# A two-layer encoder trunk: output blocks evicted later, gate rows activated together, a tenth Strassen pair, products on a constant

## The chip, the cores and the metric

One core of a Trainium2 chip runs the whole program. The metric is device time in microseconds (us); the kernel before takes 2105.63 us as the median of three runs (2105.11 to 2105.88).

## The reference

Two batches, 256 and 512 positions, go through one even and one odd layer with the same weights; together they are T = 768 rows of D = 2048. What matters here is the even layer:

```python
def _even_layer(x, g, w_in, w_out, q_gain, k_gain, sink, w_f, b_f, rel_bias):
    z = _rmsnorm(x, g) @ w_in
    q, k, v, f, ga, gf = _split(z, EVEN_SPLITS)          # 1536, 512, 512, 512, 1536, 512
    q = _rmsnorm(q.reshape(B, S, N_HEADS, HEAD_DIM), q_gain)
    k = _rmsnorm(k.reshape(B, S, N_KV_HEADS, HEAD_DIM), k_gain)
    ...
    a = _window_attention(q, k, v, rel_bias, sink) * jax.nn.silu(ga)
    fo = _fourier(f...).reshape(B, S, FOURIER_WIDTH) * jax.nn.silu(gf)
    return x + jnp.concatenate([a, fo], axis=-1) @ w_out
```

The attention looks 128 positions to either side, with 12 heads in 4 groups of 3, a bias and a sink logit. The odd layer has one input projection, a gated convolution, a spatial gate and `x + concat @ w_out` again. All is fp32.

## The kernel before

**Products.** Every fp32 operand is kept as a high and a low part: `split` (L133) casts the high part on ScalarE and subtracts it on VectorE for the low part. A product is three matmuls (`three`, L123): high by high, high by low, low by high. Operands lie with features on partitions, a row block is 128 x 768 in two halves of H = 384 columns; most matmuls are 128x128 by 128x384.

**Weights.** `Weights` holds a ring of four split weight tiles (`wh`, `wl`, 128x512), which `weights.ahead` fills a few tiles ahead, in one list `order` of all tiles of the program. For a Strassen pair `source` (L196) makes the sums of weight quarters on VectorE, in place (L204 to L210).

**Strassen pairs.** `strassen` (L486) multiplies two blocks of 128 output features by all 2048 inputs with seven products of 24 matmuls, 168 in place of 192. The first product is copied out of its bank (`r1`, L508); the others are combined by VectorE, and each of the four results goes to a *sink*: `Normed` (queries and keys), `Gates` (two blocks of the FNet gate, SiLU on ScalarE, then to memory) or `Out`.

**Order in time.** TensorE's order is the order of the Python code, with a planner on top: `Pipe` keeps a clock that each matmul moves on by its columns, generators are spawned with a delay, and `pipe.tick()` runs those that are due; `pipe.flush()` runs all that are left. The other engines get their instructions in the order in which the code issues them, moved by a framework's scheduler.

**Stages (us).** 0 to 75: the FNet projection `f`, with the rows of x loaded, split (`split_gain`, L277) and squared, the squares added on GpSimd (L559). To 165: a double block of FNet gates and the values. To 460: nine pairs `pairs_in`, eight of them queries and keys and the ninth two FNet gates. To 537: FNet, with three attention gate blocks between its products. 537 to 755: attention. To 850: four plain output blocks as two double blocks (`Out.run`, L434), then output pairs. Then the odd layer, with the same `Out.run` at 1850 to 2102.

**Attention gates.** `ga_block` (L700) multiplies one block of 128 gate features (96 matmuls), applies SiLU on ScalarE straight from the two banks (L704) and writes the row to memory. Three run in the FNet stage, nine as filler between the attention's units. The attention has 24 units (4 groups by 6 blocks of 128 queries), each a generator `attend` (L875), spawned every `UNITS_AT` = 8.0 of the planner's clock: load and split of the query (`qh`), scores with scaling (L896) and maximum, exponentials (L908, L910), division, transposes with casts (`pth`, L923), the product with the values and the copy into `at` (L933). After a group's last unit `gates` (L867) loads the three gate rows and multiplies them into `at` (`gate`).

**Output.** `Out.run` spawns `build_sums`, which makes the Strassen sums of the left operand on VectorE while the two double blocks run; after each double block it evicts its four halves at once: residual load, addition from the bank (L458), result (`keep_sum`, L952, with a square on ScalarE L958 and an addition on GpSimd L959). Then `pipe.flush()` runs what is left of the sums, and the pairs begin.

Of the kernel before, what the change touches and what calls it, by code (L numbers as in the profile page):

```python
# [17 lines left out]
P = 128  # L18
# [7 lines left out]
H = T // 2  # L26
# [16 lines left out]
FIRST_UNIT, UNITS_AT = 13.0, 8.0  # L43
PT_AT, PV_AT = 9.0, 14.2
PE = mybir.EngineType.PE
# [50 lines left out]
def trunk(ctx, tc, x_t, w_in_e, w_fn, w_vn, w_out_e, w_in_o, w_sv, w_out_o, w_f, w_st, b_s, sink, rel_bias,  # L96
# [58 lines left out]
    rr = const.tile([P, T], F32, name="rr")  # L155
    rt = const.tile([P, NT], F32, name="rt")
# [70 lines left out]
    pairs_in = [tuple(norms[i:i + 2]) for i in range(0, len(norms), 2)] + [(GF0 + 2, GF0 + 3)]  # L227
# [11 lines left out]
    order += [(w_in_e, 0, GA0 + j, q) for j in range(NQ) for q in (QLATE if j == 0 else range(4))]  # L239
# [184 lines left out]
    class Out:  # L424
# [7 lines left out]
        def run(self):  # L432
            st = Stream(self.n)

            def load(k, h, t):
                nc.sync.dma_start(out=t, in_=cat[k][:, SL[h]])

            ready = set()

            def refill(j):  # L440
                if j in ready:
                    fill(j, 1, s4d[j])
                ready.add(j)

            def done(k, s):
                if s == 1 and k < KH:
                    refill(k)

            pipe.spawn(build_sums(load, sums, BUILD, BUILD_AT, done=refill), BUILD_FROM)
            for i, tags in zip(range(0, len(PLAIN), 2), self.tags):  # L450
                duo = PLAIN[i:i + 2]
                last = i + 2 == len(PLAIN)
                st.duo(duo, tags, done if last else None, range(4) if i else self.qs)
                for b in duo:
                    for h, z in enumerate(st.take(b)):
                        res = ev()
                        nc.sync.dma_start(out=res, in_=self.res[b][:, SL[h]])
                        nc.vector.tensor_add(out=res, in0=z, in1=res)  # L458
                        self.result(b, h, res)
            pipe.flush()  # L460
            for b in self.pairs:
                self.r = [big(i)[:, :T] for i in range(2)]
                for r, c in zip(self.r, b):
                    nc.sync.dma_start(out=r, in_=self.res[c])
                lent[0] = b != self.pairs[-1]
                strassen(self.n, b, sums, ev, self, self.tags[-1])
            lent[0] = False

# [132 lines left out]
    with tc.tile_pool(name="early", bufs=1, reuse_waits="tile") as pool:  # L601
# [62 lines left out]
        class Gates:  # L664


            def keep(self, b, h, t, src=None):
                nc.scalar.activation(out=t, in_=t if src is None else src, func=AF.Silu)
                nc.sync.dma_start(out=gs_d[b - GF0][:, SL[h]], in_=t)
# [14 lines left out]
        for b in pairs_in:  # L684
            strassen(0, b, sums, ev, Gates() if b[0] >= GF0 else Normed(), (6, 2, 7, 3))
# [13 lines left out]

    def ga_block(j, tile):  # L700
        z = st.block(GA0 + j, QLATE if j == 0 else range(4))
        g = tile()
        for s in range(2):
            nc.scalar.activation(out=g[:, SL[s]], in_=z[s], func=AF.Silu)  # L704
        nc.sync.dma_start(out=ga_d[j], in_=g)

    with tc.tile_pool(name="fnet", bufs=1, reuse_waits="tile") as pool:
# [115 lines left out]
        for j in range(3):  # L823
            ga_block(j, lambda: pool.tile([P, T], F32, name="gated"))
# [3 lines left out]
    with tc.tile_pool(name="attn", bufs=1, reuse_waits="tile") as pool:  # L828
        rows.append(pool)

        class Group:


            def __init__(self, g):
                self.g = g

# [30 lines left out]
            def gates(self):  # L867
                g = self.g
                rs = []
                for j in range(3):  # L870
                    rs.append(row_tile())
                    nc.sync.dma_start(out=rs[j], in_=ga_d[3 * g + j])
                    gate(rs[j], 3 * g + j, self.at[:, j, :], g == NKV - 1)

        def attend(gr, s, qb):  # L875
# [58 lines left out]
            if (s, qb) == (1, SEQS[1][1] - 1) and g < NKV - 1:  # L934
                yield 1.0
                gr.gates()
# [8 lines left out]
        for j in range(3, NQ):  # L945
            ga_block(j, row_tile)
        pipe.flush()
        gr.gates()
# [255 lines left out]
```

## Time and profile before

| | us |
|---|---|
| median of three runs | 2105.63 |
| profiled execution | 2104.2 |
| its span | 2102.4 |
| TensorE busy | 2078.6 (99%) |
| VectorE busy | 1469.0 (70%) |
| ScalarE busy | 1000.9 (48%) |
| GpSimd busy | 75.5 (4%) |
| mean granted TensorE clock | 0.998 |

The profile is of one execution. Busy time is the union of an engine's instructions; the rest of the span the engine was idle. A row of the waits view names the engine, its line, what released it, the total, how often and the longest. In a timeline row the bracket at the end is the idle time before the instruction and what ended it; x2 joins like instructions in a row.

### The profile page before, as it was taken

The numbers are of one execution on the slowest core, as the hardware profiler recorded it, in microseconds if no ns is written. First come the engines' busy times: TensorE is split into PE (matmuls) and PEld (weight loads), VectorE is DVE, ScalarE is ACT, GpSimd is POOL, SyncE is SP. The second block draws the span as 40 slices with busy tenths as digits, with TensorE's granted clock in tenths as the row PEclk, the third lists the DMA queues.
The fourth block names the chain that finished last, engine by engine and source line by source line (L and its number), as shares of the span: only waits on it lengthen the run. The fifth ranks groups of instructions, "written<-read, shape, count | busy, mean of one in ns | idle before, by whom it ended". The sixth has DMA issues, their size and how long they took to land.

```text
span 2102.4 us, 32021 instructions
## 1 busy us (share of the span) xinstructions
PE 2078.6 (99%) x11712; PEld 2019.0 (96%) x11712; DVE 1469.0 (70%) x2605; ACT 1000.9 (48%) x1979; POOL 75.5 (4%) x75
## 2 busy tenths in 40 slices
PE   8999999999999998999999999999999999999999
PEld 6989999999999998999888999999999999999999
DVE  8686677764566787667975666666667777796665
ACT  6345545553788864335444333333334555643332
POOL 5000000000000001211000000000000000000000
PEclk9999999999999999999999999999999999999999
DMA  6895323354444385446854222222222233494342
GB/s 225 244 301 180 101 89 91 110 173 148 133 149 149 118 282 195 145 128 196 292 206 149 85 81 88 70 74 81 88 88 82 93 108 106 145 304 157 119 129 76
DMA packets 158342, 303.55 MB, mean 144 GB/s; under 512 B 16316, under 2 KB 107624, under 8 KB 158184
## 3 DMA queue, kind: packets, MB, share of 16 engines
q1 hardware_dynamic: 158184, 301.51, 44.8%
q8 instruction: 92, 1.51, 0.3%
q14 instruction: 66, 0.54, 0.1%
HBM read 240.08 MB, written 64.51 MB: 145 GB/s over the span
## 4 chain that ended last, share of the span: by engine, by line
PE 82%; DMA 6%; DVE 5%; ACT 4%; issue 2%; SPq 1%; POOL 0%; DVEq 0%; ACTq 0%; POOLq 0%
PE bank L120 82%; DMA slot<-cat 1%; DVE slot L135 1%; DVE slot L280 1%; DVE wl L135 1%; DMA wr<-in_w_out_o_dram 1%; ACT slot L134 1%; DMA xr<-in_x_t_dram 1%; PE bank L130 1%; ACT wh L134 1%; DMA s<-slot 0%; ACT slot L279 0%; ACT L704 0%; ACT sc L908 0%; DMA row<-f_d 0%
## 5 line engine op out<-in xcount | busy, mean ns | idle before, releaser
L120 PE MATMUL bank<-slot,wh 128*128 128x384 f32 x6448 | 1647.1, 336 | 5.8 <-ACT wh L134 3.6
L120 PEld LDWEIGHTS bank<-slot,wh 128*128 128x128 f32 x6448 | 1164.5, 188 | 9.6 <-ACT wh L134 3.9
L120 PE MATMUL bank<-slot,wl 128*128 128x384 f32 x3224 | 1083.9, 336 | 1.4 <-DVE wl L135 1.3
L134 ACT CAST wh<-wr 128x512 fp32r<-128x512 f32 x782 | 480.9, 621 | 722.9 <-PE bank L120 543.8
L135 DVE TENSOR_TENSOR wl<-wr,wh 128x512 fp32r<-128x512 f32 x782 | 541.3, 697 | 305.7 <-ACT wh L134 297.3
L120 PEld LDWEIGHTS bank<-slot,wl 128*128 128x128 f32 x3224 | 606.2, 188 | 2.6 <-DVE wl L135 2.6
L120 PE MATMUL bank<-wh,slot 128*128 128x512 f32 x768 | 242.2, 395 | 5.7 <-ACT slot L279 5.5
L134 ACT CAST slot<-slot 128x384 fp32r<-128x384 f32 x232 | 114.3, 515 | 171.6 <-DVE slot L135 51.1
L120 PEld LDWEIGHTS bank<-wh,slot 128*128 128x128 f32 x768 | 145.2, 189 | 38.5 <-ACT slot L279 5.5
L135 DVE TENSOR_TENSOR slot<-slot,slot 128x384 fp32r<-128x384 f32 x232 | 127.4, 555 | 47.6 <-ACT slot L134 36.3
L120 PE MATMUL bank<-wl,slot 128*128 128x512 f32 x384 | 151.5, 395 | 1.8 <-DVE wl L135 1.8
L120 PEld LDWEIGHTS bank<-wl,slot 128*128 128x128 f32 x384 | 72.7, 189 | 18.6 <-DVE wl L135 3.1
L208 DVE TENSOR_TENSOR wr<-wr 128x1024 f32<-128x1024 f32 x45 | 58.4, 1299 | 1.1
L210 DVE TENSOR_TENSOR wr<-wr 128x1024 f32<-128x1024 f32 x45 | 55.1, 1226 | 1.5
L206 DVE TENSOR_TENSOR wr<-wr 128x1024 f32<-128x1024 f32 x45 | 55.0, 1222 | 0.7
L204 DVE TENSOR_TENSOR wr<-wr 128x1024 f32<-128x1024 f32 x45 | 55.0, 1222 | 0.7
L511 DVE TENSOR_TENSOR ev<-bank,ev 128x384 f32<-128x384 f32 x45 | 25.1, 557 | 34.3 <-PE bank L120 33.9
L515 DVE TENSOR_TENSOR ev<-bank,ev 128x384 f32<-128x384 f32 x45 | 25.1, 558 | 31.8 <-PE bank L120 31.8
L520 DVE TENSOR_TENSOR ev<-ev,bank 128x384 f32<-128x384 f32 x45 | 24.9, 554 | 29.5 <-PE bank L120 29.2
L897 DVE CUSTOM_DVE_ANT_0 sc<-sc,bias 128x256 f32<-128x256 f32 (+1 forms) x72 | 31.0, 467 | 16.7 <-ACT sc L896 16.7
L959 POOL TENSOR_TENSOR rr<-rr,ev 128x384 f32<-128x384 f32 x10 | 12.0, 1201 | 806.1 <-ACT ev L958 806.1
L908 ACT ACTIVATE sc<-sc,nm 128x256 f32<-128x256 f32 (+1 forms) x72 | 38.4, 535 | 2.7 <-DVE nm L905 2.7
(196 smaller groups left out, 1439.2 us busy)
## 6 DMA issues: line engine op xcount, KB each, us to landing
wr<-in_w_in_o_dram SPq DMA_DIRECT2D x96, 512.0 KB, 3.5
wr<-in_w_in_e_dram SPq DMA_DIRECT2D x64, 512.0 KB, 3.8
slot<-cat SPq DMA_DIRECT2D x120, 192.0 KB, 4.2
wr<-in_w_out_e_dram SPq DMA_DIRECT2D x32, 512.0 KB, 3.6
wr<-in_w_out_o_dram SPq DMA_DIRECT2D x32, 512.0 KB, 3.7
slot<-x SPq DMA_DIRECT2D x64, 192.0 KB, 4.2
wr<-in_w_sv_dram SPq DMA_DIRECT2D x16, 512.0 KB, 4.9
slot<-in_x_t_dram SPq DMA_DIRECT2D x32, 192.0 KB, 4.3
```

The source lines that it names most:

```text
L120: nc.tensor.matmul(out, lhsT=lhs, rhs=rhs, start=start, stop=stop, skip_group_check=go_on)
L134: nc.scalar.copy(out=hi, in_=src)
L135: nc.vector.tensor_sub(out=lo, in0=src, in1=hi.bitcast(F32))
L204: nc.vector.tensor_sub(out=w11, in0=w12, in1=w11)
L206: nc.vector.tensor_sub(out=w11, in0=w22, in1=w11)
L208: nc.vector.tensor_sub(out=w12, in0=w22, in1=w12)
L210: nc.vector.tensor_sub(out=w21, in0=w11, in1=w21)
L511: nc.vector.tensor_add(out=u2, in0=p, in1=r1)
L515: nc.vector.tensor_add(out=r1, in0=p, in1=r1)
L520: nc.vector.tensor_sub(out=r1, in0=r1, in1=p)
L897: nc.vector.tensor_tensor_reduce(out=sj, in0=sj, in1=gr.bias[j][:, bs], scale=1.0, scalar=NEG, op0=ALU.add, op1=ALU.max, accum_out=mx[:, j ...
L908: nc.scalar.activation(out=sc[:, j, :nk * P], in_=sc[:, j, :nk * P], func=AF.Exp, bias=nm[:, j:j + 1], accum_out=den[:, j:j + 1])
```

## The change

1. **Products on a constant.** `rr` is set to 1.0 in its first half, and four fp32 matmuls of it run into bank 7 ahead of TensorE's first real product. Nothing reads them.
2. **Tenth pair.** Attention gate blocks 0 and 1 become a pair ahead of the FNet gates' pair; the sink `Gates` writes them to memory without SiLU. Blocks 2 to 4 run in the FNet stage, 5 to 11 (seven, not nine) in the attention, where units are now spawned every 6.4 of the planner's clock.
3. **SiLU three gate rows at a time.** Gate blocks are copied out of their banks by VectorE without SiLU, except block 11. `gates` loads the three rows, yields 4.0, issues three SiLUs on whole rows of 768 in a row, then the three multiplications. The last group's rows stay on the chip (`ends`); two are finished by `last_gates`, the third after the last unit.
4. **Evictions of the plain blocks.** They become generators `plain`. The first double block's are spawned 4.0 apart. For the second, `pipe.flush()` (the sums) comes first, and its four evictions are spawned 0.5 and then 4.5 apart, during the first pair.

```diff
-FIRST_UNIT, UNITS_AT = 13.0, 8.0
+FIRST_UNIT, UNITS_AT = 13.0, 6.4
+LAST_AT = 0.5
+WARM = 4
...
     rr = const.tile([P, T], F32, name="rr")
+    nc.vector.memset(rr[:, 0:H], 1.0)
+    for i in range(WARM):
+        nc.tensor.matmul(bank(7, H), lhsT=rr[:, 0:P], rhs=rr[:, 0:H], start=True, stop=True)
...
-    pairs_in = [tuple(norms[i:i + 2]) for i in range(0, len(norms), 2)] + [(GF0 + 2, GF0 + 3)]
+    pairs_in = [tuple(norms[i:i + 2]) for i in range(0, len(norms), 2)] + [(GA0, GA0 + 1), (GF0 + 2, GF0 + 3)]
...
-    order += [(w_in_e, 0, GA0 + j, q) for j in range(NQ) for q in (QLATE if j == 0 else range(4))]
+    order += [(w_in_e, 0, GA0 + j, q) for j in range(2, NQ) for q in (QLATE if j == 2 else range(4))]
...
                 st.duo(duo, tags, done if last else None, range(4) if i else self.qs)
-                for b in duo:
-                    for h, z in enumerate(st.take(b)):
-                        res = ev()
-                        nc.sync.dma_start(out=res, in_=self.res[b][:, SL[h]])
-                        nc.vector.tensor_add(out=res, in0=z, in1=res)
-                        self.result(b, h, res)
-            pipe.flush()
+                halves = [(b, h, z) for b in duo for h, z in enumerate(st.take(b))]
+                if last:
+                    pipe.flush()
+                for n, half in enumerate(halves):
+                    pipe.spawn(self.plain(*half), LAST_AT + 4.5 * n if last else 4.0 * n)
...
+        def plain(self, b, h, z):
+            res = ev()
+            nc.sync.dma_start(out=res, in_=self.res[b][:, SL[h]])
+            yield 3.0
+            nc.vector.tensor_add(out=res, in0=z, in1=res)
+            self.result(b, h, res)
...
             def keep(self, b, h, t, src=None):
-                nc.scalar.activation(out=t, in_=t if src is None else src, func=AF.Silu)
-                nc.sync.dma_start(out=gs_d[b - GF0][:, SL[h]], in_=t)
+                if b >= GF0:
+                    nc.scalar.activation(out=t, in_=t if src is None else src, func=AF.Silu)
+                elif src is not None:
+                    nc.scalar.copy(out=t, in_=src)
+                dst = ga_d[b - GA0] if b < GF0 else gs_d[b - GF0]
+                nc.sync.dma_start(out=dst[:, SL[h]], in_=t)
...
     def ga_block(j, tile):
-        z = st.block(GA0 + j, QLATE if j == 0 else range(4))
+        z = st.block(GA0 + j, QLATE if j == 2 else range(4))
         g = tile()
         for s in range(2):
-            nc.scalar.activation(out=g[:, SL[s]], in_=z[s], func=AF.Silu)
-        nc.sync.dma_start(out=ga_d[j], in_=g)
+            if j == NQ - 1:
+                nc.scalar.activation(out=g[:, SL[s]], in_=z[s], func=AF.Silu)
+            else:
+                nc.vector.tensor_copy(out=g[:, SL[s]], in_=z[s])
+        if j < NQ - 3:
+            nc.sync.dma_start(out=ga_d[j], in_=g)
+        else:
+            ends.append(g)
...
-        for j in range(3):
+        for j in range(2, 5):
...
                     nc.sync.dma_start(out=rs[j], in_=ga_d[3 * g + j])
-                    gate(rs[j], 3 * g + j, self.at[:, j, :], g == NKV - 1)
+                yield 4.0
+                for r in rs:
+                    nc.scalar.activation(out=r, in_=r, func=AF.Silu)
+                for j in range(3):
+                    gate(rs[j], 3 * g + j, self.at[:, j, :])
+
+            def last_gates(self):
+                if not self.done or len(ends) < 2:
+                    return
+                for r in ends[:2]:
+                    nc.scalar.activation(out=r, in_=r, func=AF.Silu)
+                for j, r in enumerate(ends[:2]):
+                    gate(r, 3 * self.g + j, self.at[:, j, :], True)
...
-            if (s, qb) == (1, SEQS[1][1] - 1) and g < NKV - 1:
-                yield 1.0
-                gr.gates()
+            if (s, qb) == (1, SEQS[1][1] - 1):
+                gr.done = True
+                if g < NKV - 1:
+                    yield from gr.gates()
+                else:
+                    gr.last_gates()
...
-        for j in range(3, NQ):
+        for j in range(5, NQ):
             ga_block(j, row_tile)
+            if j == NQ - 2:
+                gr.last_gates()
         pipe.flush()
-        gr.gates()
+        gate(ends[2], NQ - 1, gr.at[:, 2, :], True)
```

**How the order moves.** ScalarE in the attention, before: two SiLUs of a gate block (L704), each with its table load, around the exponentials of a unit (L908 and L910, 3 and 1 of them).

```order
L704 ACT_TABLE_LOAD
L704 ACTIVATE row<-bank 128x384
L908 ACT_TABLE_LOAD
L908 ACTIVATE sc,den<-sc,nm 128x256 x3
L910 ACTIVATE es<-es 128x3
L923 CAST pth<-bank 128x384 x2
L704 ACT_TABLE_LOAD
L704 ACTIVATE row<-bank 128x384
L134 CAST wh<-wr 128x512
L933 COPY at<-bank 128x3x128
```

After, at the first group's end: a SiLU of a whole row (L898), the exponentials (L943, L945), and the next row's SiLU behind a load again. Lines from L896 on stand 35 further down here (L943 is L908 of before).

```order
L898 ACT_TABLE_LOAD
L898 ACTIVATE row<-row 128x768
L943 ACT_TABLE_LOAD
L943 ACTIVATE sc,den<-sc,nm 128x256 x3
L945 ACTIVATE es<-es 128x3
L968 COPY at<-bank 128x3x128
L958 CAST pth<-bank 128x384 x3
L931 ACTIVATE sc<-bank,rcol 128x256 x2
L136 CAST qh<-qr 128x384
L931 ACTIVATE sc<-bank,rcol 128x256
L898 ACT_TABLE_LOAD
L898 ACTIVATE row<-row 128x768
```

The three SiLUs that stand in a row in the code stand apart here, one to a unit's exponentials.

VectorE before the first output join, before: the last four additions of the sums (L397 to L400) stand behind the weight tiles' low parts (`wl`), among the splits of the operands (L135).

```order
L135 TENSOR_TENSOR wl<-wr,wh 128x512 x2
L135 TENSOR_TENSOR slot_8917<-slot_8914,slot_8916 128x384
L397 TENSOR_TENSOR slot_9190<-slot_9189,slot_9190 128x384
L135 TENSOR_TENSOR slot_8942<-slot_8898,slot_8941 128x384
L398 TENSOR_TENSOR slot_9189<-slot_9188,slot_9189 128x384
L399 TENSOR_TENSOR slot_9188<-slot_9190,slot_9188 128x384
L135 TENSOR_TENSOR slot_8946<-slot_8899,slot_8945 128x384
L400 TENSOR_TENSOR slot_9191<-slot_9191,slot_9188 128x384
L135 TENSOR_TENSOR slot_8952<-slot_8949,slot_8951 128x384
```

After, the four additions (L402 to L405) stand together, ahead of the next weight tiles' low parts.

```order
L137 TENSOR_TENSOR wl<-wr,wh 128x512 x2
L402 TENSOR_TENSOR slot_9184<-slot_9183,slot_9184 128x384
L403 TENSOR_TENSOR slot_9183<-slot_9182,slot_9183 128x384
L404 TENSOR_TENSOR slot_9182<-slot_9184,slot_9182 128x384
L405 TENSOR_TENSOR slot_9185<-slot_9185,slot_9182 128x384
L137 TENSOR_TENSOR slot_9196<-slot_9182,slot_9195 128x384
L137 TENSOR_TENSOR slot_8883<-slot_8880,slot_8882 128x384
L137 TENSOR_TENSOR slot_8906<-slot_8903,slot_8905 128x384
L137 TENSOR_TENSOR wl<-wr,wh 128x512 x2
```

Between these additions and the low part that the first pair waits for stands one more group of weight tiles than before.

ScalarE at the same join, before: the four evictions' squares (L958) stand among the pair's weight casts, all ahead of the copy of the pair's first product (L508).

```order
L134 CAST wh<-wr 128x512
L958 ACTIVATE ev<-ev 128x384
L134 CAST wh<-wr 128x512 x2
L958 ACTIVATE ev<-ev 128x384
L134 CAST wh<-wr 128x512 x2
L958 ACTIVATE ev<-ev 128x384
L134 CAST wh<-wr 128x512 x2
L958 ACTIVATE ev<-ev 128x384
L508 COPY ev<-bank 128x384
```

After, the copy (L518) comes behind the first square (L998) alone.

```order
L136 CAST wh<-wr 128x512 x2
L998 ACTIVATE slot_9270<-ev 128x384
L136 CAST wh<-wr 128x512 x2
L518 COPY ev<-bank 128x384
L136 CAST wh<-wr 128x512
L998 ACTIVATE slot_9313<-ev 128x384
L136 CAST wh<-wr 128x512
L998 ACTIVATE slot_9358<-ev 128x384
L136 CAST wh<-wr 128x512 x4
```

The other three squares moved behind it.

## Rows read from the trace of the kernel before

**Rows 1.** Page: busy time of each engine, share of the span, instructions.

```profile
PE 2078.6 (99%) x11712; PEld 2019.0 (96%) x11712; DVE 1469.0 (70%) x2605; ACT 1000.9 (48%) x1979; POOL 75.5 (4%) x75
```

**Rows 2.** TensorE's waits: line <- releaser, us in total, times, longest.

```profile
PE bank L120 <- ACT slot L279: 5.5, 1, 5.5
PE bank L120 <- ACT wh L134: 3.6, 1, 3.6
PE bank L120 <- DVE wl L135: 3.1, 6, 1.1
PE bank L130 <- ACT at L933: 2.6, 4, 1.0
PE bank L120 <- ACT ev L508: 2.2, 1, 2.2
```

**Rows 3.** Stretch inside a pair: PE, PEld, DVE, ACT, POOL busy (count), clock, DMA, GB/s.

```profile
1160.00:1180.00 20.00, 20.00 (x117) 20.00 (x116) 15.35 (x23) 6.75 (x12) 0.17 (x3) 1.00 0.17 57
```

**Rows 4.** The same view, stretches of the first output join.

```profile
830.00:832.00 2.00, 1.92 (x6) 1.92 (x7) 1.97 (x3) 0.00 (x0) 0.89 (x1) 0.50 0.23 85
832.00:834.00 2.00, 2.00 (x11) 2.00 (x10) 1.71 (x3) 1.20 (x3) 0.01 (x1) 0.73 0.00 0
...
842.00:844.00 2.00, 2.00 (x10) 2.00 (x11) 1.62 (x3) 0.34 (x1) 0.61 (x1) 0.83 0.88 304
844.00:846.00 2.00, 2.00 (x8) 2.00 (x8) 0.69 (x1) 0.62 (x1) 0.00 (x0) 0.50 0.80 235
846.00:850.00 4.00, 4.00 (x23) 4.00 (x22) 1.23 (x2) 1.29 (x3) 0.83 (x1) 0.91 0.20 74
```

**Rows 5.** Timeline of that join: start, us, engine, line, operation, tiles, [idle <- releaser].

```profile
828.81 0.61 PE L120 MATMUL bank<-slot,wh 128*128 128x384 f32 x2 [3.63 <-ACT wh L134]
...
830.08 0.69 PE L120 MATMUL bank<-slot,wl 128*128 128x384 f32 x1 [0.66 <-DVE wl L135]
...
840.29 0.55 DVE L458 TENSOR_TENSOR ev<-bank,ev 128x384 f32<-128x384 f32 x1
...
840.92 0.52 ACT L958 ACTIVATE ev<-ev 128x384 f32<-128x384 f32 x1 [2.49 <-issue]
841.36 0.46 ACT L508 COPY ev<-bank 128x384 f32<-128x384 f32 x1
...
841.87 0.62 PE L120 MATMUL bank<-slot,wh 128*128 128x384 f32 x2 [2.18 <-ACT ev L508]
```

**Rows 6.** Windows view, the join of the second output product.

```profile
1925.00:1930.00 5.00, 4.67 (x27) 4.35 (x26) 4.66 (x8) 0.55 (x2) 0.00 (x0) 1.00 0.43 157
```

**Rows 7.** Timeline of the program's start.

```profile
9.11 1.05 PE L120 MATMUL bank<-wh,slot 128*128 128x512 f32 x2
...
11.13 0.62 PE L120 MATMUL bank<-wh,slot 128*128 128x512 f32 x2
...
18.73 6.97 DVE L280 SCALAR_TENSOR_TENSOR slot<-xr,sm,slot 128x384 fp32r<-128x384 f32 x4
...
26.36 0.50 PE L120 MATMUL bank<-wl,slot 128*128 128x512 f32 x1 [1.14 <-DVE wl L135]
```

**Rows 8.** Windows view, first to last `at` copy of the attention.

```profile
551.20:753.60 202.40, 198.82 (x1233) 196.73 (x1233) 139.25 (x450) 172.59 (x413) 0.00 (x0) 1.00 0.45 143
```

**Rows 9.** ScalarE's groups in 551.2:753.6 by form: busy, mean ns, idle before.

```profile
L134 ACT CAST wh<-wr 128x512 fp32r<-128x512 f32 x29 | 18.0, 620 | 2.2 <-PE bank L120 2.2
...
L704 ACT ACT_TABLE_LOAD x12 | 15.4, 1283 | 0.2
...
L704 ACT ACTIVATE row<-bank 128x384 f32<-128x384 f32 x15 | 7.4, 495 | 0.1
...
L134 ACT CAST vh<-row 128x768 fp32r<-128x768 f32 x3 | 2.6, 861 | 0.3 <-PE bank L120 0.3
```

**Rows 10.** ScalarE's timeline around a table load.

```profile
592.77 1.28 ACT L704 ACT_TABLE_LOAD   x1
594.07 0.49 ACT L704 ACTIVATE row<-bank 128x384 f32<-128x384 f32 x1
```

More of the change, by code (lines that the diff above doesn't have):

```diff
@@ L684, in trunk @@
         for b in pairs_in:
-            strassen(0, b, sums, ev, Gates() if b[0] >= GF0 else Normed(), (6, 2, 7, 3))
+            strassen(0, b, sums, ev, Gates() if b[0] >= GA0 else Normed(), (6, 2, 7, 3))
         pipe.flush()
@@ L698, in trunk @@
     banks["z"], banks["s"] = itertools.cycle((0, 1, 4)), itertools.cycle((6, 2, 7, 3, 5))
+    ends = []
     def ga_block(j, tile):
-        z = st.block(GA0 + j, QLATE if j == 0 else range(4))
+        z = st.block(GA0 + j, QLATE if j == 2 else range(4))
         g = tile()
         for s in range(2):
-            nc.scalar.activation(out=g[:, SL[s]], in_=z[s], func=AF.Silu)
-        nc.sync.dma_start(out=ga_d[j], in_=g)
+            if j == NQ - 1:
[6 more added lines that the diff above has]
+            ends.append(g)
     with tc.tile_pool(name="fnet", bufs=1, reuse_waits="tile") as pool:
@@ L835, in __init__ @@
                 self.g = g
+                self.done = False
             def load(self):
```

## The prediction

> **What bounds the kernel now.** I read the busy line first: TensorE works 2078.6 of the 2102.4 us [rows 1]. So the time is TensorE's work plus its 23.8 us of idle time, and a change is worth what it takes from either. The view of TensorE's waits says where the idle time lies [rows 2]: 5.5 until the first operand is there, 3.6 on a weight's cast, 2.6 in four waits in the attention, 2.2 on an eviction. The 3.6 and the 2.2 both stand in the join between the last double block and the first pair of the layer's output product, at 828 and 841 us [rows 5]. The attention, from the first `at` copy to the last, is full: 198.8 of 202.4 us, 3.6 of waits, with ScalarE at 172.6 right behind [rows 8]. There TensorE fills the time between a unit's own products with nine gate blocks.
>
> The profiled execution took 2104.2 us (span 2102.4 and 1.8 around it); the median of the three runs is 1.4 above it. I make the sum against 2104.2 and add 1.4 at the end.
>
> **The change part by part.**
>
> *Tenth pair.* Two gate blocks were 2 x 96 products; as a pair they are 7 x 24 = 168. 24 products fewer at 20.00/117 = 0.171 us each [rows 3]: **-4.1**. The pair's additions on VectorE and its weights' sums lie beside a TensorE that is the bound among the pairs (the stretch of rows 3 has no wait, VectorE at 15.35 of 20); I cost them at nothing. If that cover were gone it would show as `wl` waits of some 1 us, the longest in rows 2.
>
> *Join of the first output product.* Before, the waits are 3.63, 0.66 and 2.18 [rows 5], 6.47 in all. Behind each, TensorE's granted clock falls: 0.50 and 0.73 in 830 to 834, 0.83, 0.50 and 0.91 in 842 to 850 [rows 4]. Length times what is missing: 2 x 0.50 + 2 x 0.27 + 2 x 0.17 + 2 x 0.50 + 4 x 0.09 = 3.2. The pool is 9.7 us. The third wait is an order on ScalarE: the first product's copy `L508` stands behind the fourth eviction's square `L958` (840.92), which waits for the eviction `L458` at 840.29 [rows 5]; in the new order the copy stands ahead of three of the four squares. That wait and its half-speed stretch (2.2 + 1.7 = 3.9) should go. The first wait is a queue on VectorE: the last sums and their splits are worked off between two weight splits; in the new order the last four additions stand one weight split earlier. Five 0.55 operations less (2.75) in front of the split that TensorE needs, against 3.63 + 0.66 of waiting: I take 1.5 us as left. **-8.2**, bounds -3.9 (third wait only) and -9.7 (all). The evictions have to go somewhere: the four adds now stand in the first pair, where VectorE has time. Their result DMAs go to SP's queue with them.
>
> *Join of the second output product.* TensorE lost 0.33 us here [rows 6]; one eviction instead of four now stands ahead of the weight split: **-0.3**, bounds 0 and -0.3.
>
> *Products on a constant.* TensorE's first products run at half pace: 1.05 us for two at 9.11, 0.62 for two at 11.13 [rows 7]. About a dozen of them, 0.2 us too long each, make 2.3 us. Four products on a constant would take the slow stretch on themselves. They are fp32 of 384 columns, no row of before shows one; at four times the passes they may end up to 0.9 us after 5.53, when the first real product could start. So some 1.2 us are won by 12 us. But VectorE is behind: it works without a gap around 18.73 (four operations in 6.97 us) and TensorE waits 1.14 for its `wl` at 26.36 [rows 7]. What is won at 12 becomes waiting at 26. **-0.3**, bounds -1.0 and +0.3.
>
> *Attention.* TensorE loses filler: by the order of both kernels, 702 filler products between first and last `at` copy become 483, and the 6.4 step pulls the units together. ScalarE loses 15 SiLUs of 0.495, 9 casts of 0.62 and 3 of 23 table loads of 1.283, and gets 11 SiLUs of rows of 768 (no row; the 768-wide cast has 0.861) [rows 9]. ScalarE's rows overlap: the sum of its groups here, without loads, is 0.86 of itself in busy time, loads don't overlap. A unit's own share then is:
> - ScalarE (172.6 - 23 x 1.283 - 0.86 x (15 x 0.495 + 29 x 0.62))/23 = 5.27
> - TensorE (198.8 - 702 x 0.171)/23 = 3.43
>
> After: ScalarE 23 x 5.27 + 20 x 1.283 + 0.86 x (11 x 0.861 + 20 x 0.62) = 165.7; TensorE 78.8 + 483 x 0.171 = 161.4. **ScalarE becomes the bound**, by 4.3 us over the stretch and by more where it is bunched. The SiLUs of a group's three rows stand apart in ScalarE's order, each with its own two loads around the softmax's exponentials. Counted between successive `at` copies:
> - units 3 and 4: 5 loads, 2 row SiLUs, 1 weight cast, 39 filler: ScalarE 19.3, TensorE 13.5, +5.8
> - units 8 to 10: 6, 3, 2 and 51: 27.3 against 19.0, +8.3
> - units 18 and 19: 5, 2, 2 and 45: 19.9 against 14.6, +5.4
>
> Together 19.5. How much of this becomes waiting? The same count for before: units 5 and 6 and units 11 and 12 (4 loads, 2 SiLUs, 3 casts, 63 filler) 18.5 against 17.6, unit 14 (3, 2, 1 and 27) 10.7 against 8.0: together 4.5, and TensorE waited 3.6 there [rows 8]. At that ratio, 0.8, the new bunches cost 15.6 us of waits, 12.0 more than now: **+12.0**. Bounds: 4.3 (only the total counts, +0.7) and 24.4 (rival B, +20.8).
>
> ScalarE goes on 0.02 us after a load has ended (592.77 + 1.28, next at 594.07) [rows 10]. In the Trainium skill, "ScalarE: Activation LUTs", What ACT_TABLE_LOAD costs, each switch has another 1380 ns of drain behind the 1283 ns of load; three loads fewer would then be worth 8.0 us of ScalarE and not 3.8. The trace shows the load and not the drain, so the row decides.
>
> The last gate alone now follows the last unit, with one row in place of three; what follows it are products on other slices, and no wait of before stands there in rows 2. Nothing.
>
> **Sum:** -4.1 - 8.2 - 0.3 - 0.3 + 12.0 = -0.9, 2103.3 by the profile, **2104.7** as a median. A measurement of this kernel can tell about 0.2%, 4.2 us, from no change; with W for the waits in the attention the sum is W - 16.5, so it is faster below W = 12.3 and slower above 20.7.
>
> **The rivals.**
>
> *A, the bunches are evened out.* TensorE may run ahead between bunches: three units without loads lie between the first two, six between the second and third, and products of later gate blocks can be taken early. Then only ScalarE's total counts, W = 4.3, and the sum is -12.2: 2093.4. For it: units there have ScalarE 5.9 against TensorE about 7, so a lag is worked off. Against it: TensorE's order is fixed, and before had such free units as well and still waited 0.8 of the count.
>
> *B, slower: the bunches in full, and the clock falls behind them.* TensorE's clock fell after the waits of 3.63 and 2.18 in the join [rows 4, 5]. The three bunches would cost 5.8, 8.3 and 5.4 in waits like those. W = 19.5 and 3 x 1.6 (half of the 3.2 for each) = 24.4, the sum +7.9: 2113.5. It decides from W = 20.7: the whole count and one bunch's clock. For it: the waits are of the size that was enough in the join. Against it: the filler lies between the units' own products, so the waits may come in pieces.
>
> *C, the join doesn't gain its first wait.* The first eviction still stands ahead of the weight split on VectorE, as before, and the splits in front of that depend on loads as well as on VectorE. Then the join is worth 3.9, the sum is +3.4: 2109.0, not told from no change or just so.
>
> **How the numbers follow.** Forecast 0.40, A 0.33, B 0.19, C 0.08. The forecast's own range is W from 11 to 20 and the join from -6.5 to -9.7, 2099 to 2111; of its 0.40, 0.05 lie on the faster side and 0.03 on the slower. A is faster; B is slower; C is 0.05 the same and 0.03 slower. That makes faster 0.38, same 0.37, slower 0.25; the likeliest single case is still the forecast. The range reaches from A's 2093.4, a little lower for the bounds of the join, to a little over B: 2092.5 to 2114.0, with a good 0.8 inside.
>
> **What would show it.** TensorE's products fall by 24 at 0.171. Join: no wait over 1.5 us between the last double block and the second of the pair's products, and no stretch at 0.50. Attention: TensorE's busy time near 161 in a stretch of 174 to 180; waits named ScalarE in three bunches near the row SiLUs, 4 to 8 us each. If the stretch is under 170, A is right; with granted clock under 0.9 in it and over 182, B. Start: first wait on `wl` near 26 us is longer than 1.14. It would be wrong altogether if ScalarE's row SiLUs are far from the 0.861 of the cast, or if the join gets a wait that isn't there now, on a residual's load for an eviction.

## The result, and the profile after

The changed kernel takes 2122.43 us (median; 2120.66 to 2126.96) against 2105.65 of the kernel before on the same chip: ratio 1.0086, 95% interval 1.0074 to 1.0099. (This ratio and those below are estimated over all runs and are not quite the quotients of the medians, here 1.0080.) The forecast was 2104.7 with a range to 2114.0, so the time is outside it and on the side of rival B. The profiled execution took 2121.7 us, span 2119.9: 17.5 more than the one of before.

The page of the kernel after, its line of busy times; it answers to [rows 1]:

```profile
PE 2083.5 (98%) x11696; PEld 2017.0 (95%) x11696; DVE 1490.2 (70%) x2639; ACT 995.8 (47%) x1971; POOL 78.2 (4%) x75
```

TensorE has 24 real products fewer and is busy 4.9 us longer, and idle 36.4 us instead of 23.8. The view of TensorE's waits, kernel after, against [rows 2]:

```profile
PE bank L122 <- DVE ptl L959: 11.7, 7, 3.7
PE bank L122 <- ACT wh L136: 6.0, 2, 5.8
PE bank L122 <- DVE wl L137: 3.4, 3, 1.2
PE bank L122 <- ACT wr L553: 2.2, 1, 2.2
PE bank L122 <- ACT at L968: 2.0, 2, 1.3
```

The waits of the join are gone from the top, a wait of 5.8 us on a weight cast is new, and 11.7 us stand in seven waits on `ptl`, the low part of the transposed probabilities.

Cutting both traces at the same instructions says where the 17.5 us are (starts of the first products' copies L508/L518 and of the `at` copies, in us):

| stretch | before | after | difference |
|---|---|---|---|
| start to the first pair's copy | 182.7 | 192.0 | +9.3 |
| to the last pair's copy (8 pairs on, 9 on) | 239.8 | 268.6 | +28.9 |
| to the first `at` copy | 128.2 | 129.5 | +1.3 |
| to the last `at` copy | 202.5 | 180.4 | -22.0 |
| to the last even output pair's copy | 229.2 | 225.9 | -3.2 |
| to the first odd pair's copy | 166.1 | 169.3 | +3.2 |
| to the last output pair's copy, and the end | 954.0 | 954.1 | +0.1 |

The windows view of the attention after, first to last `at` copy, answers to [rows 8]:

```profile
590.14:770.56 180.42, 165.16 (x1012) 160.35 (x1011) 133.43 (x438) 162.05 (x390) 0.00 (x0) 0.99 0.41 128
```

TensorE 165.2 of 180.4 us, 15.3 of waits (3.6 before), ScalarE 162.1. ScalarE's groups there, by form (busy, mean ns, idle before), answer to [rows 9]:

```profile
L898 ACT ACT_TABLE_LOAD x8 | 10.3, 1283 | 1.2 <-DMA row<-ga 1.1
...
L943 ACT ACT_TABLE_LOAD x6 | 7.7, 1283 | 0.0
...
L898 ACT ACTIVATE row<-row 128x768 f32<-128x768 f32 x9 | 7.5, 844 | 0.1
L945 ACT ACT_TABLE_LOAD x4 | 5.1, 1283 | 0.1
...
L906 ACT ACT_TABLE_LOAD x2 | 2.6, 1283 | 0.0
```

Twenty loads of 1.283 us, and a row's SiLU takes 0.844. The join of the output product is nearly clean in this trace: its waits after the last `at` copy are 1.0, 0.3 and 0.2 us, and the clock stays at 1.00 where [rows 4] had 0.50 to 0.91. The windows around the pair's first products:

```profile
844.00:846.00 2.00, 2.00 (x13) 2.00 (x12) 1.42 (x3) 0.46 (x2) 0.00 (x0) 1.00 0.02 4
846.00:848.00 2.00, 0.99 (x5) 0.35 (x3) 1.91 (x4) 1.42 (x4) 0.00 (x0) 1.00 0.01 5
848.00:850.00 2.00, 1.76 (x10) 1.76 (x11) 1.97 (x3) 0.20 (x1) 1.32 (x1) 1.00 0.88 278
```

### The profile page after: what moved, and what is told of

It is laid out like the page before. It is cut to its first block, busy times and chain, and to the rows that moved or that the text cites. A ratio compares the mean times of both kernels' runs of the same rounds, so it can differ in the third digit from the quotient of the medians.

```text
span 2119.9 us, 32019 instructions
## 1 busy us (share of the span) xinstructions
PE 2083.5 (98%) x11696; PEld 2017.0 (95%) x11696; DVE 1490.2 (70%) x2639; ACT 995.8 (47%) x1971; POOL 78.2 (4%) x75
## 4 chain that ended last, share of the span: by engine, by line
PE 85%; DVE 5%; DMA 4%; ACT 4%; issue 2%; SPq 0%; POOL 0%; ACTq 0%; DVEq 0%
PE bank L122 84%; DMA xr<-in_x_t_dram 1%; DVE wl L137 1%; ACT sc L943 1%; DMA xhat<-slot 1%; DMA bias_d<-vec_d 1%; PE bank L132 1%; DMA row<-f_d 1%; DVE slot L137 1%; DVE slot L285 0%; DVE slot L1017 0%; DVE sc L949 0%; ACT wh L136 0%; ACT L898 0%; ACT slot L284 0%
## 5 line engine op out<-in xcount | busy, mean ns | idle before, releaser
L122 PEld LDWEIGHTS bank<-wl,slot 128*128 128x128 f32 x384 | 73.1, 190 | 19.2 <-DVE wl L137 3.6
L213 DVE TENSOR_TENSOR wr<-wr 128x1024 f32<-128x1024 f32 x46 | 59.7, 1298 | 1.1
L215 DVE TENSOR_TENSOR wr<-wr 128x1024 f32<-128x1024 f32 x46 | 56.4, 1226 | 1.5
L211 DVE TENSOR_TENSOR wr<-wr 128x1024 f32<-128x1024 f32 x46 | 56.9, 1237 | 0.8
L209 DVE TENSOR_TENSOR wr<-wr 128x1024 f32<-128x1024 f32 x46 | 56.2, 1222 | 0.7
L285 DVE SCALAR_TENSOR_TENSOR slot<-xr,sm,slot 128x384 fp32r<-128x384 f32 x32 | 35.5, 1156 | 18.4 <-ACT slot L284 18.4
L999 POOL TENSOR_TENSOR rr<-rr,slot 128x384 f32<-128x384 f32 x24 | 36.7, 1529 | 133.3 <-ACT slot L998 133.3
L943 ACT ACTIVATE sc<-sc,nm 128x256 f32<-128x256 f32 (+1 forms) x72 | 38.3, 535 | 1.2 <-DVE nm L940 1.1
## 6 DMA issues: line engine op xcount, KB each, us to landing
slot<-cat SPq DMA_DIRECT2D x120, 192.0 KB, 4.1
slot<-x SPq DMA_DIRECT2D x64, 192.0 KB, 4.0
slot<-in_x_t_dram SPq DMA_DIRECT2D x32, 192.0 KB, 4.0
```

The source lines that it names most:

```text
L122: nc.tensor.matmul(out, lhsT=lhs, rhs=rhs, start=start, stop=stop, skip_group_check=go_on)
L209: nc.vector.tensor_sub(out=w11, in0=w12, in1=w11)
L211: nc.vector.tensor_sub(out=w11, in0=w22, in1=w11)
L213: nc.vector.tensor_sub(out=w12, in0=w22, in1=w12)
L215: nc.vector.tensor_sub(out=w21, in0=w11, in1=w21)
L285: nc.vector.scalar_tensor_tensor(out=lo, in0=src, scalar=g, in1=hi.bitcast(F32), op0=ALU.mult, op1=ALU.subtract)
```

## The start: a load behind twelve writes

The largest miss stands where the prediction had put a term of -0.3. The timeline of SP's queue, kernel before, from 48 us:

```profile
48.38 0.42 SPq L552 DMA_DIRECT2D xr<-in_x_t_dram  x1
48.90 14.60 SPq L575 DMA_DIRECT2D bias_d<-vec_d  x12
```

and the kernel after:

```profile
46.39 14.99 SPq L585 DMA_DIRECT2D bias_d<-vec_d  x12
62.42 0.33 SPq L562 DMA_DIRECT2D xr<-in_x_t_dram  x1
```

Before, the last block of x (`xr`) is asked for ahead of the twelve writes of the attention's bias; after, it stands behind them and goes out 14.0 us later. It is also longer on its way, 9.2 us from issue to landing against 4.1 (views of the DMA issues, before and after):

```profile
xr<-in_x_t_dram SPq DMA_DIRECT2D x1, 384.0 KB, 4.1
xr<-in_x_t_dram SPq DMA_DIRECT2D x1, 384.0 KB, 9.2
```

ScalarE's timeline after shows what this held up:

```profile
71.64 1.12 ACT L284 ACTIVATE slot<-xr,sm 128x384 fp32r<-128x384 f32 x2 [19.18 <-DMA xr<-in_x_t_dram]
...
73.41 0.60 ACT L136 CAST wh<-wr 128x512 fp32r<-128x512 f32 x1
```

ScalarE sits idle for 19.2 us in front of that block's split, and the weight cast for the next product is queued behind it. TensorE's waits in order of time, and the windows around them:

```profile
74.06 0.79 PE L122 MATMUL bank<-wh,slot 128*128 128x512 f32 x1 [5.78 <-ACT wh L136]
76.05 0.79 PE L122 MATMUL bank<-wl,slot 128*128 128x512 f32 x1 [1.20 <-DVE wl L137]
```

```profile
70.00:80.00 10.00, 4.74 (x11) 3.56 (x12) 6.05 (x9) 6.71 (x11) 1.80 (x1) 0.55 0.36 128
80.00:90.00 10.00, 10.00 (x51) 8.62 (x50) 7.30 (x7) 4.30 (x8) 0.00 (x0) 0.94 0.15 58
```

A wait of 5.78 us, one of 1.20, and the granted clock at a mean of 0.55 in 70 to 80. The four products themselves, and the first wait behind them:

```profile
1.35 5.95 PE L160 MATMUL bank<-rr 128*128 128x384 f32 x8 [1.35 <-DVE rr L158]
...
7.60 0.62 PE L122 MATMUL bank<-wh,slot 128*128 128x512 f32 x2
...
21.08 0.74 PE L122 MATMUL bank<-wh,slot 128*128 128x512 f32 x2 [1.06 <-DVE slot L285]
```

They take 5.95 us. The real products begin at 6.84 (5.53 before) and soon run at full pace, 0.62 for two where [rows 7] has 1.05 at 9.11. The lead that this gives is lost again in the wait at 21.08.

**The products alone.** Added to the kernel before:

```diff
     rr = const.tile([P, T], F32, name="rr")
+    nc.vector.memset(rr[:, 0:H], 1.0)
+    for i in range(4):
+        nc.tensor.matmul(bank(7, H), lhsT=rr[:, 0:P], rhs=rr[:, 0:H], start=True, stop=True)
```

> The kernel before with one edit: the four products on a constant ahead of the first real product. Theory 1 (a queue): the products move the last x block's load in SP's queue behind the twelve bias writes, and that alone costs what the changed kernel lost up to its first pair, 9.3 us: 2115 us (2113 to 2118), with a wait of about 6 us on the weight cast near 74 us and half clock behind it. Rival (it is another part of the change, the new weight list or the tenth pair, that moved the queue, and the products are harmless): 2104 to 2106 us, no wait near 74.

Measured: 2111.57 against 2103.99, ratio 1.0038 (1.0023 to 1.0053), 7.6 us slower. SP's timeline of this kernel has the load behind the writes:

```profile
46.25 13.36 SPq L578 DMA_DIRECT2D bias_d<-vec_d  x12
60.77 0.35 SPq L555 DMA_DIRECT2D xr<-in_x_t_dram  x1
```

The first pair's copy is at 190.25 us (182.73 before), and the waits on a weight cast rose from 3.6 to 8.7 us, the longest 4.2, at 72 us. The size is a little under the 9.3 and under the expected 2113 to 2118, the place is that of theory 1: the products alone do it.

**The products, with the x load ahead.** The same, and in `prep`:

```diff
             nc.sync.dma_start(out=vec_d, in_=row)
+            yield 24.0
             for hd in range(NQ):
```

> The kernel before with the four products on a constant and one more edit: the bias writes are issued 24 later on the planner's clock, so that the last x load stands ahead of them in SP's queue again, as in the kernel before. Theory 1 (a queue): no wait near 74 us, and what is left is the worth of the products themselves: 2104.6 to 2105.8 us, the gain of some 1.2 us at 12 us eaten at the wait near 26. Rival (the products cost TensorE or VectorE time by themselves, at 5.95 us of TensorE ahead of the first real product): 2109 us or more, in spite of the queue.

Measured: 2100.87 against 2103.99, ratio 0.9987 (0.9978 to 0.9997): 2.8 us faster, a gain larger than either theory gave it. SP's timeline of this kernel:

```profile
47.98 0.33 SPq L555 DMA_DIRECT2D xr<-in_x_t_dram  x1
48.40 12.80 SPq L579 DMA_DIRECT2D bias_d<-vec_d  x12
```

The load is ahead again, the first pair's copy is at 181.66, 1.1 us earlier than before. The rival falls: with the load in its place the products cost nothing.

The 1.1 us are not the early full pace. TensorE's waits between 20 and 53 us, first of the kernel before, then of this one (the waits of 1.14 near 26 us, alike in both, left out):

```profile
20.99 0.73 PE L120 MATMUL bank<-wh,slot 128*128 128x512 f32 x2 [0.15 <-DVE slot L280]
48.02 0.50 PE L120 MATMUL bank<-wl,slot 128*128 128x512 f32 x1 [0.19 <-DVE wl L135]
52.85 0.50 PE L120 MATMUL bank<-wl,slot 128*128 128x512 f32 x1 [0.46 <-DVE wl L135]
```

```profile
20.92 0.74 PE L120 MATMUL bank<-wh,slot 128*128 128x512 f32 x2 [1.50 <-DVE slot L283]
```

At 17 us the same product runs 1.4 us earlier than before; behind the wait of 1.50 on VectorE at 20.92 it is 0.07. The 1.1 come later, where the two waits on `wl` at 48 and 53 us are gone: VectorE's order is another one there too. They are gone in the changed kernel as well.

The remaining 1.7 us of the median I can't place. The profiled execution took 2104.7 and is one of four of the ten runs that lie between 2104.3 and 2105.8; the other six lie between 2098.1 and 2102.0, and the trace can't show what these had. Nor was the `yield` put into the kernel before by itself, so how much of the 2.8 us belongs to the products isn't shown.

**The changed kernel without the products**, the four lines taken out:

> The changed kernel without the four products on a constant. Theory 1 (a queue): the last x load is ahead of the bias writes again, the start costs what it did before, 2122.4 - 9.3 = 2113.1 us (2111 to 2115), what is left over the kernel before lies in the attention. Rival (the start's loss comes from the other parts): 2120 us or more.

Measured: 2113.63 against 2103.99, ratio 1.0049 (1.0034 to 1.0064), 9.6 us slower, as theory 1 expected. First pair's copy at 182.64: the start costs what it did before.

**The changed kernel with the x load ahead** (the one line `yield 24.0`):

> The changed kernel with one edit: the bias writes are issued 24 later on the planner's clock, so that the last x load stands ahead of them in SP's queue. Theory 1 (a queue): the start's loss is gone and the four products give what they gave to the kernel before: 7 to 10 us over the kernel before, where the changed kernel had 17. Rival (in the changed kernel the start is late for another reason too): 13 us or more over it.

Measured: 2110.51 against 2103.98, ratio 1.0034 (1.0023 to 1.0046), 6.5 us slower; first pair's copy at 181.91. Theory 1 holds in both directions: some ten of the changed kernel's seventeen us are this queue. What is left of the loss has to lie behind the start.

## The late evictions

Only the change of `Out.run` with the new `plain`, on the kernel before:

```diff
+                halves = [(b, h, z) for b in duo for h, z in enumerate(st.take(b))]
+                if last:
+                    pipe.flush()
+                for n, half in enumerate(halves):
+                    pipe.spawn(self.plain(*half), LAST_AT + 4.5 * n if last else 4.0 * n)
```

> The kernel before with the late evictions alone (the last double block's four halves during the first pair). Theory (the join gains its two waits and their half-speed stretches, 8.6 us in the changed kernel's trace): 2097 us (2096 to 2099), with 1.0 to 1.5 us of waits left in the join. Rival (late evictions also make the odd layer's start late, where the changed kernel waited 2.21 us on a VALUE bank and ran at half clock behind it): 2100 to 2102 us, with that wait near 1080 us.

Measured: 2099.53 against 2103.99, ratio 0.9981 (0.9972 to 0.9990), 4.5 us faster, not 8.6. In the odd layer no wait on the values' copy stands in this kernel's view, so it isn't the rival either. The first of the join's waits stayed (view of TensorE's waits from 760 to 980 us):

```profile
PE bank L121 <- ACT wh L135: 2.9, 1, 2.9
PE bank L121 <- DVE wl L136: 0.6, 1, 0.6
```

2.9 and 0.6 in place of 3.63 and 0.66; gone are the third wait and its slow stretch. So the evictions are worth the prediction's lower bound, -3.9 (rival C's size). That the first wait is nearly gone in the changed kernel must come from its other parts. There the last `tensor_add` of the left operand's sums starts 53.1 us behind the last `at` copy, 55.8 here and 59.0 before, and in the run without the tenth pair (below) 52.0. The last group's gates are finished earlier in those two, which would start the sums earlier. TensorE also comes to the join later: 75.8 us behind the last `at` copy, 71.4 here and 72.0 before. Neither was run by itself, so this stays an argument.

The first wait also isn't the same from kernel to kernel. It is 0.26 us in the changed kernel's trace, 1.21 without the products and 1.46 with the x load ahead, where a stretch of 3.41 us at half clock follows, and between 0.6 and 1.9 in the tanh kernels and the one with the SiLU as before.

## The attention: table loads between the exponentials

The longest wait of the attention, in ScalarE's timeline of the kernel after:

```profile
650.72 1.28 ACT L898 ACT_TABLE_LOAD   x1
652.02 0.85 ACT L898 ACTIVATE row<-row 128x768 f32<-128x768 f32 x1
652.87 1.28 ACT L945 ACT_TABLE_LOAD   x1
654.16 0.20 ACT L945 ACTIVATE es<-es 128x3 f32<-128x3 f32 x1
...
656.07 1.21 ACT L958 CAST pth<-bank 128x384 fp32r<-128x384 f32 x3
...
658.05 1.28 ACT L898 ACT_TABLE_LOAD   x1
```

and in TensorE's:

```profile
658.20 0.58 PE L122 MATMUL bank<-kh,qh 128*128 128x256 f32 x1 [3.75 <-DVE ptl L959]
```

Between 650.72 and 654.16 ScalarE does one row's SiLU and two loads; the unit's exponentials, the division and the casts come behind them, VectorE's `ptl` last of all, and TensorE has waited 3.75 us. The view names VectorE, the chain ScalarE.

The same stretch in the kernel without the products, against which the next runs are read:

```profile
580.44:763.32 182.88, 167.76 (x1010) 162.89 (x1008) 133.50 (x439) 161.84 (x390) 0.00 (x0) 0.97 0.40 127
```

Its waits are 15.1 us, almost wait for wait those of the changed kernel, and it is still 2.5 us longer. The granted clock makes the difference. One stretch of each, around the same wait of 3.04 us, first the changed kernel, then the one without the products:

```profile
743.67:750.67 7.00, 5.94 (x38) 5.91 (x39) 4.84 (x18) 5.24 (x15) 0.00 (x0) 1.00 0.01 2
734.00:741.00 7.00, 5.94 (x20) 5.84 (x21) 4.00 (x14) 3.31 (x9) 0.00 (x0) 0.53 0.01 2
```

In all, the attention has 3.41 us at half clock (granted 0.50, the lower of its two levels, 1.2 GHz) in the changed kernel's trace and 10.24 in this one, as in the one with the x load ahead: 1.7 and 5.1 us lost behind almost the same waits. Of the changed kernel's four runs the profiled one has the highest mean clock, 0.996 against 0.993 to 0.995: the others lost more to the clock, where isn't shown.

**SiLU by tanh, straight from the bank.** Changed kernel without the four products, and:

```diff
-            if j == NQ - 1:
-                nc.scalar.activation(out=g[:, SL[s]], in_=z[s], func=AF.Silu)
-            else:
-                nc.vector.tensor_copy(out=g[:, SL[s]], in_=z[s])
+            nc.scalar.activation(out=g[:, SL[s]], in_=z[s], func=AF.Tanh, scale=0.5)
+            nc.vector.scalar_tensor_tensor(out=g[:, SL[s]], in0=g[:, SL[s]], scalar=1.0, in1=z[s],
+                                           op0=ALU.add, op1=ALU.mult)
```

with the same in the pair's sink, the factor 0.5 in `gate`, and no SiLU on rows: x (1 + tanh(x/2)) / 2 is SiLU.

> The changed kernel without the four products, and with the attention gates' SiLU written as x (1 + tanh(x/2)) / 2: the tanh on ScalarE straight from the bank, the rest on VectorE. The tanh lies in the same table set as the exponential, so the order has no table load between the first and the last `at` copy (20 before). Tenth pair and 6.4 spacing stay. Theory 2 (the attention's waits come from ScalarE, above all from the row SiLUs with two loads each between a unit's exponentials): ScalarE's time there falls from 162 to some 134 us, the waits from 15 to under 4, the stretch from 182.9 to 163-167, and the time comes to 8 us under the kernel before (6 to 10). Rival (the units follow each other too closely at 6.4, each unit's own chain of scores, exponentials, transposes is longer than the filler beside it): waits stay at 10 or more and the time 2 us or more over the kernel before.

Measured: 2093.28 against 2103.2, ratio 0.9943 (0.9926 to 0.9959), 9.9 us faster. The windows view of its attention:

```profile
581.18:741.61 160.43, 159.98 (x1010) 158.38 (x1009) 133.02 (x438) 132.07 (x369) 0.00 (x0) 1.00 0.46 144
```

Waits of 0.45 us at the same 6.4 spacing, 160.4 us where the kernel without the products has 182.9. The spacing isn't it.

**SiLU as before the change, with the tenth pair.** Changed kernel without the four products, SiLU straight from the bank in the pair's sink too, none on rows, and:

```diff
-            if j == NQ - 1:
-                nc.scalar.activation(out=g[:, SL[s]], in_=z[s], func=AF.Silu)
-            else:
-                nc.vector.tensor_copy(out=g[:, SL[s]], in_=z[s])
+            nc.scalar.activation(out=g[:, SL[s]], in_=z[s], func=AF.Silu)
```

> The changed kernel without the four products, and with the SiLUs as in the kernel before: straight from the bank, two of 384 a block, none on rows; tenth pair and 6.4 spacing stay. The order has 14 table loads in the attention, not 20. Theory 2 (loads and row SiLUs on ScalarE make the waits): ScalarE by the count 155 us against TensorE's 161, waits of 4 to 9 us in place of 15, so 3 us over the kernel before to 3 under it. Rival (spacing, not ScalarE): waits stay at 12 to 16, 8 us or more over the kernel before.

Measured: 2101.38 against 2103.2, ratio 0.9994 (0.9984 to 1.0003). Its attention:

```profile
580.44:751.78 171.34, 164.07 (x1012) 160.51 (x1011) 131.36 (x435) 149.97 (x384) 0.00 (x0) 0.99 0.43 136
```

1.8 us faster, not told from no change. 7.3 us of waits with 14 loads, as expected, and ScalarE at 150.0, under the 155 of the count. 20, 14 and 0 loads give 15.1 (the kernel without the products), 7.3 and 0.45 us of waits.

**Loads or row operations?** Changed kernel without the four products, rows of 768 activated at the end of a group as there, but by the tanh form:

```diff
+        def soft(r):
+            th = pool.tile([P, T], F32, name="th")
+            nc.scalar.activation(out=th, in_=r, func=AF.Tanh, scale=0.5)
+            nc.vector.scalar_tensor_tensor(out=r, in0=th, scalar=1.0, in1=r, op0=ALU.add, op1=ALU.mult)
```

> The changed kernel without the four products, with the gate rows still activated as rows of 768 at the end of a group, but by the tanh form: ScalarE keeps an operation of 768 for each row at the same places, and the order has no table load between the first and the last `at` copy (20 before). It separates the loads from the row operations. Theory 2a (the loads make the waits): ScalarE some 136 us, waits under 3, stretch 161 to 165, 6 to 10 us under the kernel before. Rival 2b (the 768-wide operations in the middle of a unit's exponentials make them): waits of 7 or more, stretch 169 or more, the kernel before plus or minus 3.

Measured: 2097.45 against 2103.98, ratio 0.9973 (0.9959 to 0.9987), 6.5 us faster. Its attention:

```profile
579.63:744.62 164.99, 161.75 (x1007) 159.25 (x1005) 140.94 (x447) 135.75 (x371) 0.00 (x0) 0.99 0.44 140
```

3.2 us of waits with ScalarE at 135.8, just over what theory 2a set, far from 2b: of the 15.1 the loads make 11.9, and at most 2.8 is left for the row operations (0.45 without both). In the Trainium skill, "ScalarE: Activation LUTs", Table sets: the hidden batching unit, exponential and tanh stand in one set and calls should be grouped by set. The traces agree: twenty loads in the changed kernel, where SiLU and exponential alternate although the code has three SiLUs in a row, and none between the `at` copies of the tanh kernels. Three SiLUs in one instruction on one tile of three rows were not tried.

**Without the tenth pair**, spacing 8.0 again, row SiLUs kept, no products:

```diff
-... + [(GA0, GA0 + 1), (GF0 + 2, GF0 + 3)]
+... + [(GF0 + 2, GF0 + 3)]
...
-        for j in range(5, NQ):
+        for j in range(3, NQ):
```

> The changed kernel without the four products, without the tenth pair and with 8.0 spacing: nine gate blocks in the attention again, but with the SiLUs on rows of 768; 17 table loads in the attention. Theory 2: TensorE has its 199 us of filled work against some 160 on ScalarE, waits of 2 to 6 us as before, so the kernel is 4 to 9 us faster than the kernel before, all of it from the join. Rival (the row SiLUs and the VectorE copies alone make the loss, whatever the filler): waits of 10 or more, no gain on the kernel before.

Measured: 2095.19 against 2103.2, ratio 0.9958 (0.9943 to 0.9973), 8.0 us faster. Its attention has 201.2 us, 198.9 of them TensorE's:

```profile
550.54:751.78 201.24, 198.88 (x1232) 196.87 (x1231) 145.31 (x465) 167.65 (x405) 0.00 (x0) 1.00 0.43 139
```

The row SiLUs add no waits while nine blocks fill TensorE: 2.4 us, 3.6 before. What made them dear was taking the filler away; the spacing, which went back with it, did no harm in the tanh form. The gain of this run lies behind the attention: 221.2 us from the last `at` copy to the last even pair's, 229.2 before.

**The parts put together.** The same with the products and the x load ahead:

> The changed kernel without the tenth pair and with 8.0 spacing, and with the bias writes issued 24 later: the late evictions, the SiLUs on rows and the four products, each where it does no harm. Expected: the gain of the run without pair and products (8.0 us) and 1 to 2.8 us of the start: 9 to 11 us under the kernel before. If the start's gain is eaten later, 8 us.

Measured: 2092.61 against 2103.98, ratio 0.9944 (0.9926 to 0.9962), 11.4 us faster, 0.4 more than expected. And the tanh form with the tenth pair, the products and the x load ahead:

> The kernel of the tanh form with the four products back and the bias writes issued 24 later, so that the last x load stays ahead of them in SP's queue. Theories 1 and 2: the start gains what it did in the run with the x load first, 1 to 2.8 us on the tanh form: 9 to 12 us under the kernel before. Rival (the start's gain is eaten later): the same as the tanh form within 1 us.

Measured: 2091.39 against 2103.2, ratio 0.9940 (0.9925 to 0.9954), 11.8 us faster. Its median is 1.9 us under that of the tanh form alone, within what the runs of either spread; the two combined kernels can't be told from each other.

## Why the prediction was wrong, point by point

- **The start (forecast -0.3, bounds -1.0 and +0.3; measured +9.3).** This is the step that failed. It costed the four products on TensorE and VectorE and named no queue. The products moved the order of SP's queue, where the last x load and twelve bias writes changed places; the order of SP's instructions would have shown it. The bounds came from the nearest waits of TensorE and couldn't hold a load that goes out 14 us late. The part that it did reason about was right: the lead is lost in waits on VectorE, as it said, at 21 us already. What the products gain with the load in its place, 1.1 us at the first pair, are two waits on `wl` at 48 and 53 us, which it didn't have.
- **The attention (forecast +12.0; waits 15.3 - 3.6 = +11.7, but the stretch +15.9).** The waits have the forecast size, in part by luck. The factor 0.86 for ScalarE's overlap stands in the totals and was left out of the bunches; with it the new bunches come to 18.2 and the old ones to 3.4, the ratio is 1.05 and not 0.8, and the waits would have been put at some 19. Bunch by bunch 4.6, 6.6 and 4.3 were forecast and 2.8, 4.7 and 5.0 measured (611.9 and 620.4, 658.2 and 667.7, 733 to 745 us); 2.6 more stand outside them. ScalarE 165.7 was forecast, 162.1 measured; TensorE 161.4, and 160.0 in the tanh kernel with the same products. What the term left out is the clock behind the waits: the stretch was 177.0 forecast and 180.4 measured, 1.7 of it half speed for 3.41 us behind the 3.75 wait. In the run without the products, with almost the same waits, the term by the same count (224 products fewer) is +18.7, 5.1 of it half speed. The view named VectorE's `ptl`, not ScalarE.
- **The first join (forecast -8.2; measured -8.6 in the changed kernel: waits 6.8 to 1.4 and the 3.2 of slow clock).** The size is right, and half of its reason isn't the evictions, as the run with them alone shows (-4.5). It is partly luck too: with the x load ahead the same join keeps 2.5 us of waits and 1.7 of slow clock.
- **The tenth pair (-4.1)** is right as a count; what it does to the filler is the attention's term.
- **The second join (-0.3)**: the wait of 0.33 [rows 6] is gone.
- **Not in the sum: the odd layer's start, +3.2.** TensorE waits 2.21 us for a copy out of a bank (`wr`, 1094 us) and has half speed behind it. The kernel before with the products and the x load ahead has the same stretch at 169.0 us and a wait of 2.2, the other kernels have it between 164.7 and 167.9. Most of the others have the same wait, from 0.3 to 2.15 us, without the half speed, and the kernel before, the evictions alone and the changed kernel without the products have none. So no single part of the change decides it. SP's loads and writes there go out a little differently from kernel to kernel; which of them decides wasn't tested, and it stays open.

With the measured terms, -4.1 + 9.3 + 15.9 (stretch, with the 222 products of filler fewer at 0.171 taken off) - 8.6 - 0.3 + 3.2 + 0.4 (waits before the attention) = 15.8 of the 17.5.

Rivals: B was half right. The count didn't come in full (15.3 of waits, not 19.5), and the largest miss, at the start, wasn't B's. But the clock does fall behind the bunches: B put it at 4.8, and it is 1.7 in the changed kernel's trace and 5.1 in those without the products and with the x load ahead. Without the queue the changed kernel is 6.5 us slower than before; on 2105.65 that is 2112.2, above the forecast's own range and nearer to B's 2113.5 than to the forecast. A fell: the bunches weren't evened out. C's price is what the evictions alone are worth.

## What to carry to other kernels

An instruction that costs nothing on its engine can still move the order of every queue: compare the order of the DMA queue too, and look for a load that has changed places with a burst of writes. Taking work off the bound engine in a stage is worth something only as long as the next engine isn't the bound there; count both per stretch and per bunch before moving filler out. A wait is priced by its length and by the clock behind it, and the second part differed between traces with almost the same waits (1.7 and 5.1 us), so one trace doesn't give it. Activations that share a table set with their neighbours remove the loads altogether, which no order in the code guaranteed here.

## What the runs showed of the hardware that was not expected

Writing one function by a formula that stays in the softmax's table set took ScalarE from 162 to 132 us in the attention and turned the change's loss into a gain. The four fp32 products of 384 columns took 5.35 to 6.77 us at the start, the whole of it or its greater part before the granted clock first rose to its upper level. It rose between 4.9 and 11.2 us with them and between 8.8 and 11.1 without, so in one kernel they didn't bring it forward at all. Almost the same waits in the attention came with 3.41 or 10.24 us at half clock. The kernel before itself had medians of 2103.2 to 2105.65 us on the chips used, so each ratio is to its runs on the same chip.
